# Whole float32 weights for the first expert, and a skipped branch behind its down product

## The chip, the core and the metric

The kernel runs on one core of a Trainium2 chip. A core has a matmul engine (PE, with a weight-load side PEld), a vector engine (DVE), an activation engine (ScalarE, ACT), a general engine (GpSimd, POOL), a sequencer that mostly issues transfers (SyncE, SP) and 16 DMA engines. Each engine works through its own list of instructions in order and waits on semaphores for the others. The metric is the time of one execution on the device in microseconds (us), the median of several runs.

## What is computed

Two encoder layers over 512 tokens of width 1024. Each has a norm, an input projection, four attention mixers, an output projection with a residual, and then a mixture of 16 experts, which is where the change is made. Cut to that part:

```
for layer in range(2):
    ...                                     # norm, projection, four mixers, residual
    t = rms_norm(x, norm2_g)                # 512 x 1024
    g_prob = softmax(t @ wg + bg)           # 4 groups, the best one is taken
    e_logits = (t @ we + be) of that group  # 4 experts, the best two are taken
    gate = weight of each of the 16 experts for each token
    for e in range(16):
        hid = silu(t @ w_gate[e]) * (t @ w_up[e])     # 1024 -> 512
        y = y + gate[:, e:e+1] * (hid @ w_down[e])    # 512 -> 1024
    x = x + y
```

Everything is float32.

## The kernel before, in words

**Tokens.** The routed tokens of an expert are gathered into a list of at most 96 (`CAP`). A list is made from one-hots (`oh`, DVE) and four small matmuls (`pli`), then GpSimd gathers the rows (`xg`) from a copy of `h` in memory (`h2d`), PE transposes them (`ptg`, eight of them, L1413) and they become `xh` and `xl`. Expert 0 is an exception: its input comes out of PE already transposed, from products of one-hots with `h` (`acc`, L1142). If an expert had more than 96 tokens, further rounds would follow in `overflow` (L1466): a number of rounds (`nrd`) is read by every engine, and a branch (L1478) is entered if it is over 1. With these inputs it is never entered.

**Weights.** An expert has 12 units of 512 KB (128 x 1024 float32): four of gate (`g`), four of up (`u`), four of down (`d`). `Weights.load` puts them in order on SP's queue into raw buffers (26 of them, and rows of `x_sb` when these are free). `Weights.split` makes two operands of a unit in the one-pass matmul format float32r: `hi` is a rounded copy (ACT, L144), `lo` what is left (`raw - hi`, DVE or GpSimd, L145); the raw buffer is free after `lo`. Six split units can stand at a time (`HL`): a unit's slot comes free when PE has used it (`free`). `mm3` (L268) multiplies in three one-pass matmuls: hi by `xh`, lo by `xh`, hi by `xl`, so a unit takes 6 matmuls of 512 columns.

**Order.** The units follow the list `MOE_ORDER`: 0g 0u 1g 0d 1u 2g 1d 2u 3g 2d and so on: gate of the next expert before down of this one. In the loop (L1536 to L1585) a unit is split if that has not been done, used, freed, and then further units are split up to six ahead. `silu` (ACT, L1427) follows the gate units, `hidden` (DVE, L1439, the product `sg` of silu and up) the first gate unit of the next expert, `turn_hidden` (L1448) its third; `turn` of the next expert stands inside up, and so do the list (`listed`, `start`) of the expert three ahead. `store` (ACT, L1462) scales the down product into `ye`, which GpSimd adds to the output.

**The opening.** What stands between the router and the first expert is written out by hand in `TAIL`, a table of words for each stage. The letters that matter here: `s` splits the next unit (`sV` with DVE, `sG` with GpSimd for `lo`), `T` makes expert 0's input from `acc`, `K` computes the routing weights (`weights`) and their parts, `m` clears a gather buffer, `S` starts the gather of expert 1, `O` is the overflow branch, `B` and `q` are a store and a small copy. The last stage, 69, is `T K m sG B O q sG S`. So the branch is passed before any expert, and expert 1's gather comes last.

Of the kernel before, what the change touches and what calls it, by code (L numbers as in the profile page):

```python
# [11 lines left out]
FT = mybir.dt.float32  # L12
# [7 lines left out]
S = 512  # L20
# [31 lines left out]
HOLD = 2  # L52
MIX = "gg" + "dg" * 8 + "gggggg"
# [9 lines left out]
def hybrid_encoder(ctx: ExitStack, tc: tile.TileContext, I: dict, out: bass.AP, depth=2, dbg=None):  # L63
# [83 lines left out]
    class Weights:  # L147
# [4 lines left out]
        def __init__(self):  # L152
            self.spec, self.raw, self.hl, self.where = [], {}, {}, {}
            self.loaded = self.done = self.used = 0
            self.moe_pools = []
            self.held, self.paused = 0, False
            self.spare, self.spare_upto = [], 0

# [30 lines left out]

        def split(self, upto, E=V):  # L190

            while self.done < min(upto, self.loaded) and self.done < self.used + self.HL - self.held:
# [5 lines left out]
                r = self.where.pop(u)  # L198
                if isinstance(r, bass.AP):
                    self.spare.append(r)  # L200
# [13 lines left out]
        def free(self, upto):  # L214
            for u in range(self.used, upto):
                del self.hl[u]
            self.used = upto
# [105 lines left out]
    for layer in range(depth):  # L323
# [32 lines left out]
        with ExitStack() as c2:  # L356
# [431 lines left out]
            with ExitStack() as c3:  # L788
# [356 lines left out]
                def list_rows():  # L1145

                    pl = ps.tile([128, 512], FT, name="pli", tag="tr")
                    for t in range(NT):
# [7 lines left out]
                              p=route, x=pick, s=lambda E: W.split(W.done + 1, E), w=warm)  # L1156
# [151 lines left out]
        with ExitStack() as c2:  # L1308
# [30 lines left out]
            def weights():  # L1339
# [17 lines left out]
                W.load(len(W.spec), A)  # L1357
# [20 lines left out]
            class Expert:  # L1378
# [5 lines left out]
                def lists(self, parts, rows=True, gates=True):  # L1384

                    c0, c1 = 0 if rows else 2, 5 if gates else 2
                    pl = pq.tile([128, 8], FT, name="pli", tag="pv")
# [16 lines left out]
                def turn(self, turned=None):  # L1404
                    self.xh = sm.tile([128, 8, CAP], FR, name="xh", bufs=2)
                    self.xl = sm.tile([128, 8, CAP], FR, name="xl", bufs=2)
                    for k in range(0, 8, 4):
                        if turned:
                            pt = turned[k // 4]
                        else:  # L1410
                            pt = ps.tile([128, 4, CAP], FT, name="ptg", tag="tr")
                            for j in range(4):
                                PE.transpose(pt[:, j], self.g[:CAP, (k + j) * 128:(k + j + 1) * 128], ident[:CAP, :CAP])  # L1413
# [52 lines left out]
            def overflow():  # L1466
# [11 lines left out]
                with tc.If(rounds > 1):  # L1478
                    V.memset(off, 0.0)
                    SP.dma_start(posd[0].rearrange("(t p) e -> p t e", p=128), pos)  # L1480
                    SP.dma_start(posd[1].rearrange("(t p) e -> p t e", p=128), gate)
                    with tc.For_i(1, rounds):
                        V.tensor_scalar(off, off, float(CAP), None, op0=OP.add)
                        with tc.For_i(0, NE) as e:
                            one = bass.ds(e, 1)
                            pe_ = sm.tile([128, 2, NT], FT, name="pe")
                            for j in range(2):
                                SP.dma_start(pe_[:, j], posd[j, :, one].rearrange("(t p) o -> p (t o)", p=128))
# [6 lines left out]
                            x.lists(lambda t: co[:, t])  # L1495
# [3 lines left out]
                            x.pg = ps.tile([128, FF], FT, name="pg", tag="mm")[:CAP]  # L1499
                            x.pu = pq.tile([128, FF], FT, name="pu", tag="pv")[:CAP]  # L1500
# [9 lines left out]

                            x.pd = [pool.tile([128, 512], FT, name="pd", tag=tag)[:CAP] for pool, tag in ((ps, "mm"), (pq, "pv"))]
# [10 lines left out]
            def start(e):  # L1522
# [3 lines left out]
                else:  # L1526
# [5 lines left out]
                          m=lambda: G.memset(xg[1], 0.0), S=lambda: start(1), K=weights, O=overflow,  # L1532
                          q=lambda: G.tensor_copy(parts[..., :2], tokb[:, :, None].to_broadcast([128, NT, NE, 2])))
            tail(TAIL[len(seq) + 5])
            for e, m in MOE_ORDER:
                us = wbase[layer, e, m][0]  # L1536
                for i, u in enumerate(us):
# [24 lines left out]
                    for s, todo in ((e + 3, (('u', 0), ('u', 2))),) + (((2, (('g', 2), ('u', 0))),) if e == 0 else ()):  # L1562
                        if (m, i) in todo and s < NE:
                            (start if (m, i) == todo[1] else listed)(s)
                    if (e, m) == (0, 'u') and i in (0, 2):
                        j = i // 2
                        X[j].hots = hots(j, sm.tile([128, NT, CAP], BF, name="oh", bufs=2))
                        X[j].lists(lambda t: parts[:, t, j], rows=j == 0)
# [111 lines left out]
```

## Time and profile before

| | us |
|---|---|
| runs: median (lowest, highest) of 3 | 1391.43 (1387.01, 1392.2) |
| profiled execution, its own time | 1387.39 |
| its span, first to last instruction | 1385.6 |
| PE busy | 1293.8 (93%) |
| DVE busy | 1087.5 (78%) |
| ACT busy | 876.4 (63%) |
| GpSimd busy | 358.5 (26%) |

All times in the trace count from the start of the span. The expert phases run from about 386 to 700 us and from 1062 to the end. A row of the timeline has a start, a duration, the engine, the line of the kernel, the operation, what it writes and reads, and a count; in brackets stands how long the engine had been idle and who released it. Consecutive instructions of one kind are put together, and their durations overlap, so that the distance between two is the difference of two starts. A row of stretches has the busy time of PE, PEld, DVE, ACT and GpSimd with instruction counts, then the granted clock of PE as a share of full speed, the share of the DMA engines' time and the GB/s. A row of the chain has a start, a duration and the work on which the end depended. A busy engine may be one whose instruction waits inside.

### The profile page before, as it was taken

The page shows a single profiled execution, that of the slowest core. Times are in us where ns is not written, and L with a number is a line of the kernel's source. Part 1 is how long each engine was busy: PE and PEld are TensorE (multiplying, and loading weights), DVE is VectorE, ACT ScalarE, POOL GpSimd, SP SyncE. Part 2 cuts the span into 40 slices and gives each one's busy share as a digit, 9 for nine tenths or more (in the row PEclk, how much of TensorE's full clock was granted, in tenths as well). Part 3 has the DMA queues.
Part 4 walks back from the last instruction along what each step waited for, and adds up shares of the span by engine and source line. Part 5 has one row for each costly group of instructions (what it writes and reads, how often), then busy time and mean ns, then how long its engine had stood idle before and what let it go on. Part 6 is the DMA issues. An engine that isn't in the chain of part 4 may idle for free.

```text
span 1385.6 us, 21247 instructions
## 1 busy us (share of the span) xinstructions
PE 1293.8 (93%) x7222; PEld 1013.9 (73%) x7222; DVE 1087.5 (78%) x2108; ACT 876.4 (63%) x1439; POOL 358.5 (26%) x582
## 2 busy tenths in 40 slices
PE   8998899999969999999989998999998899999996
PEld 6776688888836666766777886888886566667674
DVE  4636776878688999999876488687876799999994
ACT  3443357766357888888744454676644588888884
POOL 4204324323422111111041152431345021111120
PEclk8999999999979999999999999999997899999999
DMA  7332251012699999999454223200176899999960
GB/s 198 116 97 62 83 177 51 18 60 108 257 334 292 370 363 373 359 361 332 124 136 123 91 77 79 69 28 28 62 296 222 292 351 368 370 363 366 367 206 13
DMA packets 100575, 278.46 MB, mean 201 GB/s; under 512 B 19465, under 2 KB 30521, under 8 KB 100456
## 3 DMA queue, kind: packets, MB, share of 16 engines
q1 hardware_dynamic: 89528, 247.95, 50.4%
q0 software_dynamic: 10352, 27.41, 7.9%
q10 hardware_dynamic: 576, 1.64, 0.4%
q8 instruction: 59, 0.97, 0.3%
q14 instruction: 60, 0.49, 0.1%
HBM read 264.34 MB, written 24.81 MB: 209 GB/s over the span
## 4 chain that ended last, share of the span: by engine, by line
PE 25%; DVE 17%; DMA 12%; issue 11%; ACT 4%; POOL 1%; POOLq 0%; DVEq 0%; ACTq 0%; SPq 0%
PE pm L268 9%; DVE lo L145 7%; PE pd L268 5%; DMA raw<-in_expert_w_down_dram 4%; DMA raw<-in_expert_w_gate_dram 3%; PE ptr L276 2%; DMA raw<-in_expert_w_up_dram 2%; PE pv L911 2%; PE pu L268 2%; ACT hi L144 2%; PE pg L268 2%; DMA out_dram<-ye,ix 1%; DVE oh L341 1%; ACT ye L1462 1%; DVE xl L145 1%
## 5 line engine op out<-in xcount | busy, mean ns | idle before, releaser
L145 DVE TENSOR_TENSOR lo<-raw,hi 128x1024 fp32r<-128x1024 f32 (+2 forms) x400 | 483.6, 1230 | 68.1 <-ACT hi L144 58.3
L144 ACT ACTIVATE hi<-raw 128x1024 fp32r<-128x1024 f32 (+1 forms) x410 | 422.7, 1050 | 92.6 <-PE pu L268 20.2
L268 PE MATMUL pm<-lo,hTh 128*128 128x512 f32 (+2 forms) x384 | 137.3, 358 | 6.8 <-DVE lo L145 5.1
L268 PE MATMUL pm<-hi,hTh 128*128 128x512 f32 (+2 forms) x384 | 139.3, 363 | 3.0 <-ACT hi L144 1.5
L268 PE MATMUL pm<-hi,hTl 128*128 128x512 f32 (+2 forms) x384 | 136.9, 356 | 0.4
L268 PE MATMUL pg<-lo,xh 128*96 128x512 f32 x256 | 104.0, 406 | 5.5 <-POOL lo L145 4.0
L268 PE MATMUL pu<-hi,xh 128*96 128x512 f32 (+1 forms) x272 | 109.0, 401 | 0.0
L268 PE MATMUL pg<-hi,xh 128*96 128x512 f32 x256 | 106.2, 415 | 2.4 <-ACTq L1478 1.4
L268 PE MATMUL pd<-hi,hl 128*96 128x512 f32 x256 | 102.1, 399 | 4.5 <-DVE hl L145 4.5
L268 PE MATMUL pu<-lo,xh 128*96 128x512 f32 (+1 forms) x272 | 105.7, 388 | 0.0
L268 PE MATMUL pu<-hi,xl 128*96 128x512 f32 (+1 forms) x272 | 104.8, 385 | 0.0
L911 PE MATMUL pv<-v,pT 128*128 128x64 f32 x768 | 98.3, 271 | 6.5 <-DVE pT L899 2.7
L268 PE MATMUL pg<-hi,xl 128*96 128x512 f32 x256 | 102.9, 402 | 0.6 <-DVE E L1349 0.6
L268 PE MATMUL pd<-lo,hh 128*96 128x512 f32 x256 | 101.2, 395 | 1.6 <-DVE lo L145 1.6
L882 ACT ACTIVATE p<-p,m 128x512 f32<-128x512 f32 x96 | 68.7, 716 | 52.2 <-DVE m L864 51.9
L911 PEld LDWEIGHTS pv<-v,pT 128*128 128x128 f32 x768 | 93.5, 192 | 10.8 <-DVE pT L899 4.8
L268 PE MATMUL pd<-hi,hh 128*96 128x512 f32 x256 | 100.7, 394 | 0.0
L268 PEld LDWEIGHTS pm<-lo,hTh 128*128 128x128 f32 x384 | 73.5, 191 | 18.2 <-DVE lo L145 9.8
L268 PEld LDWEIGHTS pm<-hi,hTh 128*128 128x128 f32 x384 | 73.8, 192 | 15.4 <-ACT hTh L144 2.4
L268 PEld LDWEIGHTS pm<-hi,hTl 128*128 128x128 f32 x384 | 73.5, 192 | 11.2 <-DVE hTl L145 2.1
L276 PE MATMUL ptr<-ident,p 128*128 128x128 f32 x512 | 76.9, 272 | 0.3
L276 PEld LDWEIGHTS ptr<-ident,p 128*128 128x128 f32 x512 | 63.3, 140 | 17.8 <-DVE pT L899 1.2
(371 smaller groups left out, 2746.6 us busy)
## 6 DMA issues: line engine op xcount, KB each, us to landing
raw<-in_expert_w_down_dram SPq DMA_DIRECT2D x116, 512.0 KB
raw<-in_expert_w_gate_dram SPq DMA_DIRECT2D x114, 512.0 KB
raw<-in_expert_w_up_dram SPq DMA_DIRECT2D x112, 512.0 KB
raw<-in_w_in_dram SPq DMA_DIRECT2D x32, 512.0 KB
raw<-in_w_out_dram SPq DMA_DIRECT2D x16, 512.0 KB
toep<-brep SPq DMA_DIRECT2D x16, 448.0 KB
x_sb<-in_expert_w_gate_dram SPq DMA_DIRECT2D x14, 512.0 KB
x_sb<-in_expert_w_down_dram SPq DMA_DIRECT2D x12, 512.0 KB
```

The lines of the kernel that those rows point to most:

```text
L144: A.activation(hi, src, AF.Copy)
L145: E.tensor_tensor(lo, src, hi.bitcast(FT), op=OP.subtract)
L268: PE.matmul(pt, a, b, start=first and n == 0, stop=last and n == tot - 1)
L276: PE.transpose(pt[:c, i * 128:(i + 1) * 128], s, ident)
L341: V.tensor_scalar(oh[:, t], iota, pos[:, t, e:e + 1], None, op0=OP.is_equal)
L882: A.activation(p, p, AF.Exp, bias=m, scale=-1.0, accum_out=s)
L911: PE.matmul(st['pv'][:, t], self.pT[:, k * 128:(k + 1) * 128], self.v(k), start=k == 0, stop=k == NT - 1)
L1462: A.activation(ye[:CAP, n * 512:(n + 1) * 512], self.pd[n], AF.Copy, scale=self.w)
```

## The change

Three things are done.

1. The eight units of expert 0's gate and up are kept whole (`W.whole`): they are not split, PE multiplies the raw float32 buffer with a float32 `xh`, one matmul where there were three. `xl` of expert 0 is gone; its `xh` is two plain copies, one by ACT and one by DVE. A raw buffer of such a unit is free when PE has used it.
2. The branch is taken out of `TAIL` and stands behind expert 0's down product, `store` included; expert 1's silu comes behind it. Its inner loads are issued by ACT and not SP, and its PSUM tags change.
3. The order of the opening is changed: in stage 69 the gather of expert 1 comes first, then expert 0's input, six splits on DVE (1g and the first two of 0d) and then the routing weights; the single splits of stages 64 and 66, and all GpSimd splits of stage 69, are gone. The first lists are spread by a table `FIRST`, and the gate weights of experts 0 and 1 are listed within their own down units.

```diff
-        64: "sV d0",
+        64: "d0",
-        66: "e1 sG c2",
+        66: "e1 c2",
-        69: "T K m sG B O q sG S"}
+        69: "m S T B sV sV sV sV sV sV K q"}
+FIRST = ((2, ((0, 'u', 1), (0, 'u', 3))), (3, ((1, 'g', 1), (1, 'g', 3))), (4, ((1, 'u', 0), (1, 'u', 2))))
...
+        def next(self):
+            while self.done in self.whole and self.done < self.loaded:
+                src, k, n, moe = self.spec[self.done]
+                self.hl[self.done] = self.raw.pop(self.done).rearrange("p (k n) -> p k n", k=k)
+                self.done += 1
+            return self.done
...
         def free(self, upto):
             for u in range(self.used, upto):
                 del self.hl[u]
+                if u in self.whole:
+                    self.leave(u)
+                    self.load(len(self.spec))
...
+                if e == 0:
+                    W.whole.update(wbase[l, e, m][0])
...
+                    if turned:
+                        self.xh = self.xh.bitcast(FT)
+                        A.activation(self.xh[:, :4], turned[0], AF.Copy)
+                        V.tensor_copy(self.xh[:, 4:], turned[1])
+                        return
...
+                    if self is X[0]:
+                        for j in range(2):
+                            k = 2 * i + j
+                            PE.matmul(getattr(self, 'p' + m), self.xh[:, k], w[:, j], start=k == 0, stop=k == 7)
+                        return
...
-                    SP.dma_start(r, w)
+                    A.dma_start(r, w)
...
-                    for s, todo in ((e + 3, (('u', 0), ('u', 2))),) + (((2, (('g', 2), ('u', 0))),) if e == 0 else ()):
+                    for s, todo in FIRST if e < 2 else ((e + 3, (('u', 0), ('u', 2))),):
...
-                    if (e, m) == (0, 'u') and i in (0, 2):
+                    if m == 'd' and e < 2:
...
-                if m == 'g':
+                if m == 'g' and e != 1:
                     X[e].silu()
...
+                if (e, m) == (0, 'd'):
+                    overflow()
+                    X[1].silu()
```

The order of instructions on PE where the expert phase of a layer opens, before. `nrd` is the number of rounds, and between the two branch rows lies the body that is not entered; `pg` is the gate product, `raw` a whole unit, `hi` and `lo` its two parts.

```order
L1142 MATMUL acc<-scr,h_4155 128x96 x8
L1469 TENSOR_LOAD nrd
L1478 COMPARE_AND_BRANCH
...
L1478 UNCONDITIONAL_BRANCH
L268 MATMUL pg<-hi,xh 96x512
L268 MATMUL pg<-lo,xh 96x512
L268 MATMUL pg<-hi,xl 96x512
```

The same place of PE now; `ptg` are the transposes of expert 1's gathered rows, `pli` the list of expert 2.

```order
L1163 MATMUL acc<-scr,h_4149 128x96 x8
L1450 MATMUL pg<-raw,xh 96x512 x8
L1450 MATMUL pu<-raw,xh 96x512 x4
L1438 MATMUL ptg<-ident,xg 128x96 x8
L1450 MATMUL pu<-raw,xh 96x512 x4
L1411 LDWEIGHTS oh
L1411 MATMUL pli<-parts,oh 96x5
```

The branch is gone from between `acc` and the first gate product, and 16 matmuls with whole weights stand for 48 with halves.

ACT at its branch, before: the last rows ahead of it, and the first behind it. `DMAHW` names are the eight lanes on which loads report.

```order
L1356 ACTIVATE e_4320<-e_4320 128x4 [waits DVE_49]
L186 DMA x_sb<-in_expert_w_up_dram 128x1024 [waits DMAHW7_49,DMASW3_49]
L144 ACTIVATE hi<-raw 128x1024 [waits DMAHW6_49]
L1469 TENSOR_LOAD nrd [waits DVE_49]
L1478 COMPARE_AND_BRANCH
...
L1478 UNCONDITIONAL_BRANCH [waits Activation_49]
L144 ACT_TABLE_LOAD
L144 ACTIVATE hi<-raw 128x1024
```

ACT at its branch now, behind the down product of expert 0; `ye` is that product scaled, `sg<-pg` the silu of expert 1, `xh<-ptg` the input of expert 2.

```order
L145 ACTIVATE hi<-x_sb 128x1024 [waits DMAHW1_49,DVE_49,PE_49]
L1492 ACTIVATE ye<-pd,w 96x512 [waits DMASW1_49,DMASW0_49,DMASW2_49,DVE_49,PE_49]
L1492 ACTIVATE ye<-pd,w 96x512 [waits PE_49]
L1499 TENSOR_LOAD nrd [waits DVE_49]
L1508 COMPARE_AND_BRANCH
...
L1508 UNCONDITIONAL_BRANCH [waits Activation_49]
L1457 ACTIVATE sg<-pg 96x512 [waits DMAHW3_49,DMAHW2_49,DMAHW4_49,DMAHW1_49,DMAHW5_49,DMAHW0_49,DMAHW6_49,DVE_49,DMAHW7_49,PE_49,Activation_49]
L145 ACTIVATE hi<-x_sb 128x1024
L145 ACTIVATE hi<-raw 128x1024 [waits PE_49]
L145 ACTIVATE xh<-ptg 128x384 [waits PE_49] x2
```

Behind the branch there were splits of expert 0's units; now there is a silu that has all eight lanes in its wait.

SP at its branch now (before it had the same rows with the branch at L1478, behind the loads of two up units).

```order
L185 DMA raw<-in_expert_w_down_dram 128x1024 [waits DMAHW5_49,DVE_49]
L185 DMA x_sb<-in_expert_w_down_dram 128x1024 [waits DMAHW6_49,DVE_49]
L1499 TENSOR_LOAD nrd [waits DVE_49]
L1499 ISA x2
L1508 COMPARE_AND_BRANCH
...
L1508 UNCONDITIONAL_BRANCH [waits DMAHW0_49,DMAHW1_49,DMAHW2_49,DMAHW3_49,DMAHW4_49,DMAHW5_49,DMAHW6_49,DMAHW7_49]
L185 DMA x_sb<-in_expert_w_down_dram 128x1024 [waits DMAHW7_49,DVE_49]
L185 DMA raw<-in_expert_w_down_dram 128x1024 [waits DMAHW0_49,DVE_49]
```

The wait for the eight lanes came with the branch; the loads ahead of it are now ones that wait for DVE.

## Rows read from the trace of the kernel before

**Rows 1.** The page: busy time of engines, and two groups of instructions.

```profile
PE 1293.8 (93%) x7222; PEld 1013.9 (73%) x7222; DVE 1087.5 (78%) x2108; ACT 876.4 (63%) x1439; POOL 358.5 (26%) x582
...
L145 DVE TENSOR_TENSOR lo<-raw,hi 128x1024 fp32r<-128x1024 f32 (+2 forms) x400 | 483.6, 1230 | 68.1 <-ACT hi L144 58.3
L144 ACT ACTIVATE hi<-raw 128x1024 fp32r<-128x1024 f32 (+1 forms) x410 | 422.7, 1050 | 92.6 <-PE pu L268 20.2
```

**Rows 2.** Stretches, from layer 0's first expert to its last ones.

```profile
386.00:396.00 10.00, 6.46 (x13) 3.24 (x13) 9.19 (x24) 7.36 (x10) 5.44 (x4) 0.51 1.01 375
...
462.34:480.62 18.28, 18.09 (x89) 12.68 (x89) 16.98 (x24) 15.13 (x19) 2.75 (x2) 1.00 1.01 367
663.42:681.70 18.28, 18.28 (x89) 13.02 (x88) 16.50 (x17) 15.66 (x20) 1.44 (x1) 1.00 0.40 111
```

**Rows 3.** The chain of waits, two experts' down products near layer 0's end.

```profile
662.51 5.53 PE pd L268 x24
...
680.14 5.53 PE pd L268 x24
```

**Rows 4.** The timeline of PE, opening of the experts in both layers.

```profile
383.85 2.10 PE L1142 MATMUL acc<-scr,h 128*128 128x96 f32 x16
...
392.96 0.74 PE L268 MATMUL pg<-lo,xh 128*96 128x512 f32 x1 [1.70 <-POOL lo L145]
...
407.98 0.78 PE L1389 MATMUL pli<-parts,oh 128*96 128x5 bf16 x4 [3.28 <-DVE oh L341]
...
419.34 0.59 PE L268 MATMUL pg<-hi,xh 128*96 128x512 f32 x1
...
430.95 0.40 PE L268 MATMUL pu<-hi,xh 128*96 128x512 f32 x1
...
1058.76 3.71 PE L1142 MATMUL acc<-scr,h 128*128 128x96 f32 x16
...
1069.32 0.74 PE L268 MATMUL pg<-lo,xh 128*96 128x512 f32 x1 [1.73 <-POOL lo L145]
...
1074.73 0.57 PE L268 MATMUL pg<-hi,xh 128*96 128x512 f32 x1
...
1094.13 0.63 PE L268 MATMUL pg<-hi,xh 128*96 128x512 f32 x1
```

**Rows 5.** PE's timeline, the same transposes in windows ending at 374.6 and 374.9.

```profile
374.44 0.41 PE L276 MATMUL ptr<-ident,x_sb 128*128 128x128 f32 x2
...
374.44 0.63 PE L276 MATMUL ptr<-ident,x_sb 128*128 128x128 f32 x4
```

**Rows 6.** SP's waits at the branch: 384 to 404 and 1062 to 1080.

```profile
SPq L1478 <- SPq L1478: 5.9, 4, 2.4
...
SPq L1478 <- SPq L1478: 6.8, 1, 6.8
```

**Rows 7.** The timeline of ACT, silu of expert 0 in layer 0.

```profile
400.57 1.28 ACT L1427 ACT_TABLE_LOAD   x1 [1.88 <-SPq L1478]
401.86 0.59 ACT L1427 ACTIVATE sg<-pg 96x512 f32<-96x512 f32 x1
```

**Rows 8.** The chain of waits, three loads: start, us to landing.

```profile
586.40 3.28 DMA raw<-in_expert_w_up_dram
...
1066.52 6.41 DMA raw<-in_expert_w_up_dram
...
1219.52 13.89 DMA raw<-in_expert_w_down_dram
```

**Rows 9.** The timeline of DVE: routing weights' end, expert 1's sequence, both anchors.

```profile
390.33 0.26 DVE L1334 CAST parts<-gate 128x64 bf16<-128x64 f32 x1
...
432.94 1.23 DVE L145 TENSOR_TENSOR lo<-x_sb,hi 128x1024 fp32r<-128x1024 f32 x1 [0.86 <-ACT hi L144]
...
439.46 0.68 DVE L1439 TENSOR_TENSOR sg<-sg,pu 96x512 f32<-96x512 f32 x1
...
1114.73 0.68 DVE L1439 TENSOR_TENSOR sg<-sg,pu 96x512 f32<-96x512 f32 x1
```

More of the change, by code (lines that the diff above doesn't have):

```diff
@@ L157, in __init__ @@
             self.spare, self.spare_upto = [], 0
+            self.whole = set()
         def add(self, src, k, n, moe=False):
@@ L188, in load, with room_for, leave @@
                 self.loaded += 1
+        def room_for(self):
+            return sum(u not in self.whole for u in range(self.used, self.done)) < self.HL - self.held
+        def next(self):
[4 more added lines that the diff above has]
+            return self.done
+        def leave(self, u):
+            r = self.where.pop(u)
+            if isinstance(r, bass.AP):
+                self.spare.append(r)
         def split(self, upto, E=V):
-            while self.done < min(upto, self.loaded) and self.done < self.used + self.HL - self.held:
+            while self.next() < min(upto, self.loaded) and self.room_for():
                 u = self.done
@@ L1155, in hybrid_encoder @@
                 STAGES = dict(l=list_rows, b=norm_pair, c=turn_pair, o=open_out, d=close_out, e=turn_x, r=norm_x, f=logits, h=normed,
-                              p=route, x=pick, s=lambda E: W.split(W.done + 1, E), w=warm)
+                              p=route, x=pick, s=lambda E: W.split(W.next() + 1, E), w=warm)
                 def tail(words):
@@ L1356, in weights @@
                 A.activation(e2, e2, AF.Exp)
-                W.load(len(W.spec), A)
+                W.load(len(W.spec))
                 gw = sm.tile([128, NT], FT, name="gw")
@@ L1382, in __init__, with lists @@
                     self.g, self.hots = g, hots
-                def lists(self, parts, rows=True, gates=True):
+                def lists(self, parts, rows=True, gates=True, room=None):
                     c0, c1 = 0 if rows else 2, 5 if gates else 2
-                    pl = pq.tile([128, 8], FT, name="pli", tag="pv")
+                    pool, tag = room or (pq, "pv")
+                    pl = pool.tile([128, 8], FT, name="pli", tag=tag)
                     for t in range(NT):
@@ L1405, in turn @@
                     self.xh = sm.tile([128, 8, CAP], FR, name="xh", bufs=2)
+                    if turned:
[3 more added lines that the diff above has]
+                        return
                     self.xl = sm.tile([128, 8, CAP], FR, name="xl", bufs=2)
                     for k in range(0, 8, 4):
[L1408 to L1413, printed above, removed]
+                        pt = ps.tile([128, 4, CAP], FT, name="ptg", tag="tr")
+                        for j in range(4):
+                            PE.transpose(pt[:, j], self.g[:CAP, (k + j) * 128:(k + j + 1) * 128], ident[:CAP, :CAP])
                         split(self.xh[:, k:k + 4], self.xl[:, k:k + 4], pt)
@@ L1479, in overflow @@
                     V.memset(off, 0.0)
-                    SP.dma_start(posd[0].rearrange("(t p) e -> p t e", p=128), pos)
-                    SP.dma_start(posd[1].rearrange("(t p) e -> p t e", p=128), gate)
+                    A.dma_start(posd[0].rearrange("(t p) e -> p t e", p=128), pos)
+                    A.dma_start(posd[1].rearrange("(t p) e -> p t e", p=128), gate)
                     with tc.For_i(1, rounds):
@@ L1494, in overflow @@
                                        [one_hot(pe_[:, 0, t:t + 1]) for t in range(NT)])
-                            x.lists(lambda t: co[:, t])
+                            x.lists(lambda t: co[:, t], room=(ps, "tr"))
                             V.memset(x.g, 0.0)
@@ L1509, in overflow @@
                             x.turn_hidden()
-                            x.pd = [pool.tile([128, 512], FT, name="pd", tag=tag)[:CAP] for pool, tag in ((ps, "mm"), (pq, "pv"))]
+                            x.pd = [pq.tile([128, 512], FT, name="pd", tag="sc")[:CAP] for _ in range(2)]
                             for n in range(2):
@@ L1531, in hybrid_encoder @@
             STAGES.update(T=lambda: X[0].turn(late['acc']), B=lambda: G.dma_start(stream[:, NT - 1], x_sb[:, NT - 1]),
-                          m=lambda: G.memset(xg[1], 0.0), S=lambda: start(1), K=weights, O=overflow,
+                          m=lambda: G.memset(xg[1], 0.0), S=lambda: start(1), K=weights,
                           q=lambda: G.tensor_copy(parts[..., :2], tokb[:, :, None].to_broadcast([128, NT, NE, 2])))
@@ L1561, in hybrid_encoder @@
                         X[e + 1].turn()
-                    for s, todo in ((e + 3, (('u', 0), ('u', 2))),) + (((2, (('g', 2), ('u', 0))),) if e == 0 else ()):
-                        if (m, i) in todo and s < NE:
-                            (start if (m, i) == todo[1] else listed)(s)
-                    if (e, m) == (0, 'u') and i in (0, 2):
-                        j = i // 2
-                        X[j].hots = hots(j, sm.tile([128, NT, CAP], BF, name="oh", bufs=2))
-                        X[j].lists(lambda t: parts[:, t, j], rows=j == 0)
+                    for s, todo in FIRST if e < 2 else ((e + 3, (('u', 0), ('u', 2))),):
+                        if e > 1:
+                            todo = [(e,) + w for w in todo]
+                        if (e, m, i) in todo and s < NE:
+                            (start if (e, m, i) == todo[1] else listed)(s)
+                    if m == 'd' and e < 2:
+                        if i == 0:
+                            X[e].hots = hots(e, sm.tile([128, NT, CAP], BF, name="oh", bufs=2))
+                        elif i == 2:
+                            X[e].lists(lambda t: parts[:, t, e], rows=e == 0)
                     if m == 'g' and i == 0 and e == NE - 1 and not last:
```

9 lines of the change are left out of this document (3 added, 6 removed).

## Prediction

> **What bounds the kernel now.** I read the page's busy shares first: the matmul engine PE is busy 93% of the span [rows 1], which says little about where an edit would pay. So I cut the first expert phase into stretches [rows 2]. From 386 to 396 us PE is busy only 6.46 of 10 us, at a granted clock of 0.51, the lower of its two levels (1.2 GHz of 2.4), while VectorE (DVE) is busy 9.19. In the steady part each expert takes 18.28 us. PE looks full there (18.09), but the page warns that a busy PE may be one that waits, so I set its work against the end of the layer, where the chain of waits holds PE alone: from one expert's 24 down matmuls at 662.51 to the next one's at 680.14 it takes 17.63 us [rows 3]. The steady period, 0.65 us longer, is thus set by DVE's chain of `lo` subtractions and the gate product `sg`; time that the start of the phase saves is kept only if it brings DVE's sequence forward. My anchor is DVE's `sg` of expert 1 (silu times up): 439.46 us in layer 0, 1114.73 in layer 1 [rows 9]. From there on both kernels run the same program, so the shifts of the anchors are what the change is worth.
>
> Before the anchor PE waits for the operands of expert 0: for GpSimd's `lo` 1.70 us at 392.96, for one-hots 3.28 us at 407.98. Expert 1's first gate matmul comes at 419.34 (layer 1: 1094.13), its up at 430.95 [rows 4]. The phase opens at 386.0, where the 16 `acc` pieces (383.85 + 2.10) end.
>
> **The change, part by part.** *Expert 0 whole.* It removes 48 one-pass matmuls and 8 splits (8 `hi` of ScalarE, ACT; 8 `lo`, two of them on GpSimd), and puts 16 ordinary float32 matmuls of 512 columns in their place. No such matmul is in the trace. `acc` is one with 96 columns; its 8 matmuls per half stand as 16 pieces, so I take two passes. Two more 128-column float32 transposes cost 0.63 - 0.41 = 0.22 us [rows 5], 0.11 each; four times that is 0.44 for 512 columns, 0.88 a matmul in two passes, 14.1 us for 16. The bounds: one pass would cost 7.0; `acc`'s 2.10 / 16 = 0.131 per 96 columns, scaled by columns, gives 0.70 a pass and 22.4 us. I take 14.1, because in `acc` weight loads of 128 columns stand beside short passes, and a pass of 512 columns covers them.
>
> The Trainium skill weighs against this: "TensorE: Matmul & The Clock Gate", the table of terms, calls the transpose mode four times faster for FP32. If plain passes took four times what the transposes of the trace take, the 16 would cost an estimated 56 us; `acc` with 0.131 us for 96 columns [rows 4], hardly more than a transpose, speaks against it, so I give that no chance.
>
> The clock: `acc` takes 3.71 us in layer 1, where the clock is low, against 2.10 [rows 4]; matmuls of 512 columns I take at double, 1.76. In layer 1 the matmuls came back to full at 1074.73, 5.4 us after the last wait of over a microsecond, which ended at 1069.32 [rows 4]. After the change PE has no operand to wait for: the raw units have long landed, and `xh` needs two plain copies. I take 6 us at the low level: 6 / 1.76 = 3.4 matmuls, then 12.6 x 0.88 = 11.1, together 17.1. With eight transposes of xg (0.9 by the same 0.11) and four list matmuls (0.2) expert 1's gate starts 18.2 after the opening, at 404.2 instead of 419.34. Gate 1 and down 0 took 430.95 - 419.34 = 11.6; with two more list groups (0.3) they end at 416.1. The six splits ahead (6 x 1.23 on DVE [rows 1]) and the routing weights behind them (they ran from 387 to past 390.33 [rows 9], some 5 us with their parts) end near 399 and hide behind the float32 matmuls; the first to need them is the list of expert 2 near 404, so their cover is 5 us.
>
> *The branch moved.* It is never entered, yet each engine loads a number and jumps. SP, which issues the weight loads, must also see its outstanding loads land before it may pass: 5.9 us of waits in layer 0, 6.8 in layer 1 [rows 6], and ACT's silu waited for it, 1.88 us [rows 7]. The change puts the inner loads on ACT's queue, but in the new order SP's row behind the branch still waits for all eight load lanes, and so does ACT's silu of expert 1. Queued behind that silu on ACT are the next `hi` and the transposed input; behind those DVE's `lo`, one-hots, `xl` and the anchor, and PE's list matmuls within up 1. How late is the silu? DVE's last `lo` before the branch is that of 2g0: its slot comes free with the third unit of down 0, near 414.6, and `hi` 1.05 and `lo` 1.23 [rows 1] end it near 417.2. It frees the buffer of the last load, issued near 417.5. At the branch of layer 1 a load took 6.41 us to land; in the steady parts one took 3.28 and one 13.89 [rows 8]. I take 4.8, the middle of 6.41 and 3.28, since SP's queue is thin while it waits for buffers. So SP and ACT go on near 422.6, with a guess of 0.3 for the jump. ACT's own road, two `ye` and the branch behind 416.1, ends near 419.6: the drain comes last.
>
> For the same time the Trainium skill has a sum: "DMA: Bandwidth & Descriptors", on the two cost components, 2.0 us plus bytes over 436 GB/s, an estimate of 3.2 us for 512 KB. By that the silu comes 1.6 us earlier in each layer and the total 3 us lower; the 6.41 us [rows 8] speaks against it.
>
> From silu to anchor: silu 0.59, one `hi` 1.05, then DVE's sequence that the trace has in the same order, 439.46 - 432.94 = 6.5 [rows 1, 7, 9]; 8.2 in all. Anchor 0 comes at 430.8 instead of 439.46: 8.7 gained. Layer 1 opens at 1058.76 + 3.71 = 1062.5; the same steps give gate 1 at 1080.7 (against 1094.13), down 0's end at 1092.6, the silu at 1099.1, the anchor at 1107.3 against 1114.73: 7.4 gained. PE idles some 4 us at the list matmuls while ACT waits and may lose its clock by that; I charge 0.5 us a layer, as DVE and not PE sets the pace.
>
> *The rest.* Loads that PE now releases come no later than DVE released them. PE's own jump I charge at nothing, since PE waits behind it anyway; without that cover it is a fraction of a microsecond. The spread lists and the lost GpSimd splits take work off DVE's crowded start and cost nothing.
>
> **Sum:** 8.7 + 7.4 - 1.0 = 15.1 us, 1.1%. On the profiled execution of 1387.39 (span 1385.6) that is 1372; on the median of the runs, 1391.43, 4 us above it, which I forecast for, 1376.
>
> **The rivals.** (a) *The drain costs little.* If the last load lands in 3.28 us or goes out before `lo` of 2g0, the silu comes at ACT's own 419.6, 3 us earlier a layer; with a clock that rises 2 us sooner (1 us a layer) it is 8 in all: gain 23, 1368. For it: the 3.28. Against: the 6.41, measured at the branch.
> (b) *The drain is as long as the longest landings.* Ten us instead of 4.8 takes 5.2 a layer; gain 5, 1386. For it: 13.89. Against: the 6.41, again.
> (c) *The gain is not kept.* SP, held at the branch, issues late, and splits wait for loads later: 1391. Against: by 663 to 682 us the DMA share has fallen to 0.40 [rows 2], so loads run well ahead.
> (d) *The other side: the clock stays low through the whole float32 stretch.* PE is fed without a gap, but float32 passes may not raise its clock: in layer 1 `acc` ran 3.71 us without a gap and did not. Then 16 x 1.76 = 28.2 us instead of 17.1, 11.1 later a layer: layer 0 loses 2.4, layer 1 3.7, and the low clock that runs on into gate 1 some 1.5 each. 9 us in all, 1400. It decides from 21 to 23 us of low clock: the stretch takes 14.1 + t/2 with t us at the low level, and the gains of 7.4 and 8.7 are gone 14.8 and 17.4 us past the 6. For it: that row. Against: `acc` at 383.85 and the transposes at full clock [rows 4, 5].
> That the change doesn't do what it says has no weight: the new order has the 16 matmuls, and the branch behind down 0.
>
> **How the numbers follow.** Forecast 0.54, (a) 0.20, (b) 0.11, (c) 0.06, (d) 0.09. A measurement of this kernel can tell about 0.5%, 7 us, from no change. Faster by more: the forecast and (a), 0.74; within: (b) and (c), 0.17; slower: (d), 0.09. The range goes from (a) taken from the profiled execution and one us more, 1363, to (b), 1387; above it lie (c) and (d), 0.15, below it 0.05. The 22.4 us bound of the float32 price would cost 8 us a layer and land at (c).
>
> **What would show it.** Right: `pg` and `pu` pieces 0.44 us apart after some 6 us at twice that; gate 1 near 404 and 1081; SP waiting about 5 us at the branch and ACT's silu 6 us behind down 0; anchors near 431 and 1107; the period still 18.28. Wrong: all pieces at 0.88 (d), no wait of ACT at the branch (a), one of 10 us (b), `hi` waiting for loads or a longer period (c).

## The result and the profile after

The changed kernel takes 1396.88 us (median of 12 runs) against 1390.01 for the kernel before (12 runs): a ratio of 1.0061, 95% interval 1.0050 to 1.0071. It is slower by 0.6%. The forecast was 1376, with a range of 1363 to 1387: wrong in sign and outside the range. The profiled execution has a span of 1393.8 us, 8.2 more than before.

The first step held to within 1.5 us. PE's timeline of the changed kernel (start, duration, engine, line, operation, count; in brackets idle time and who ended it), layer 0 and then layer 1:

```profile
385.39 2.00 PE L1163 MATMUL acc<-scr,h 128*128 128x96 f32 x16
387.23 7.03 PE L1450 MATMUL pg<-raw,xh 128*96 128x512 f32 x16
394.10 3.60 PE L1450 MATMUL pu<-raw,xh 128*96 128x512 f32 x8
401.28 1.51 PE L1438 MATMUL ptg<-ident,xg 96*128 96x96 f32 x8 [3.59 <-DMA xg<-h2d,nrd]
402.58 4.62 PE L1450 MATMUL pu<-raw,xh 128*96 128x512 f32 x8
...
407.21 0.45 PE L289 MATMUL pg<-hi,xh 128*96 128x512 f32 x1
...
419.71 0.44 PE L289 MATMUL pu<-hi,xh 128*96 128x512 f32 x1 [0.36 <-PEq L1508]
...
438.25 0.78 PE L1411 MATMUL pli<-parts,oh 128*96 128x5 bf16 x4 [13.49 <-DVE oh L362]
...
1063.78 3.71 PE L1163 MATMUL acc<-scr,h 128*128 128x96 f32 x16
1067.29 8.50 PE L1450 MATMUL pg<-raw,xh 128*96 128x512 f32 x16
...
1084.35 0.46 PE L289 MATMUL pg<-hi,xh 128*96 128x512 f32 x1
...
1116.27 0.78 PE L1411 MATMUL pli<-parts,oh 128*96 128x5 bf16 x4 [14.43 <-DVE oh L362]
```

The 16 pieces of `pg` take 7.03 us, from 387.23 to the first of `pu` at 394.10 (0.43 each, 0.86 a matmul), at the full clock. Expert 1's first gate matmul stands at 407.21 (419.34 before, [rows 4]) and its up at 419.71 (430.95). Counted from the end of `acc`, the gate comes 13.6 us earlier in layer 0 and 14.8 in layer 1. Then the line of `pli` in up 1 says where all of it went: PE sits idle 13.49 us, and 14.43 in layer 1, waiting for DVE's one-hots. DVE in turn waits for ACT, and then come the anchors, the `sg` of expert 1 (DVE's timeline):

```profile
436.79 1.23 DVE L146 TENSOR_TENSOR lo<-x_sb,hi 128x1024 fp32r<-128x1024 f32 x1 [16.22 <-ACT hi L145]
...
443.31 0.68 DVE L1469 TENSOR_TENSOR sg<-sg,pu 96x512 f32<-96x512 f32 x1
...
1121.32 0.68 DVE L1469 TENSOR_TENSOR sg<-sg,pu 96x512 f32<-96x512 f32 x1
```

The anchors are at 443.31 and 1121.32, where the forecast had 430.8 and 1107.3 and the kernel before 439.46 and 1114.73 [rows 9]. ACT, in the same two places:

```profile
419.52 1.26 ACT L1492 ACTIVATE ye<-pd,w 96x512 f32<-96x512 f32 x2 [0.71 <-PEq L1508]
435.22 0.59 ACT L1457 ACTIVATE sg<-pg 96x512 f32<-96x512 f32 x1 [14.44 <-SPq L1508]
...
1113.24 0.59 ACT L1457 ACTIVATE sg<-pg 96x512 f32<-96x512 f32 x1 [15.31 <-SPq L1508]
```

Behind the two `ye` ACT is idle 14.44 us and 15.31 us ahead of the silu of expert 1, released by SP at the branch (L1508). Before, the silu at the branch waited 1.88 us [rows 7]. SP's own timeline shows why it takes so long:

```profile
395.16 3.39 SPq L188 DMA_DIRECT2D raw<-in_expert_w_gate_dram  x4
400.04 5.61 SPq L185 DMA_DIRECT2D raw<-in_expert_w_down_dram  x4
407.51 4.18 SPq L188 DMA_DIRECT2D raw<-in_expert_w_up_dram  x4
413.11 5.23 SPq L188 DMA_DIRECT2D raw<-in_expert_w_gate_dram  x4
419.15 0.33 SPq L185 DMA_DIRECT2D raw<-in_expert_w_down_dram  x1
420.60 17.79 SPq L185 DMA_DIRECT2D x_sb<-in_expert_w_down_dram  x2
```

SP issues its last load ahead of the branch at 420.60; ACT's silu starts at 435.22. So that load, and those still under way in front of it, took 14.6 us to land, where the forecast took 4.8. How much was under way stands in the DMA view of a stretch (packets, MB and share of the 16 engines' time of `q1`, the queue of SP's loads). The first row is the changed kernel from that load to the silu; the other two are the kernel before, from the last load ahead of its branch to the end of SP's waits there (392.94 to 400.4 us in layer 0, 1069.29 to 1077.6 in layer 1):

```profile
q1 hardware_dynamic: 957, 3.46, 63.4%
...
q1 hardware_dynamic: 427, 1.55, 59.9%
...
q1 hardware_dynamic: 369, 1.32, 48.6%
```

With 0.52 MB to a unit, 6.6 units still had to move in the changed kernel, and 3.0 and 2.5 in the kernel before. The stretches of the changed kernel (busy time of PE, PEld, DVE, ACT, GpSimd; then the granted clock, the DMA share and the GB/s):

```profile
386.00:396.00 10.00, 10.00 (x34) 4.66 (x33) 8.62 (x18) 6.38 (x8) 2.98 (x3) 1.00 0.99 381
396.00:406.00 10.00, 6.41 (x18) 3.00 (x17) 5.11 (x23) 3.06 (x5) 0.00 (x0) 0.83 1.02 376
406.00:420.00 14.00, 13.64 (x69) 9.03 (x68) 10.89 (x26) 8.29 (x9) 2.27 (x2) 1.00 1.03 382
420.00:438.00 18.00, 4.76 (x26) 3.22 (x24) 1.78 (x3) 3.56 (x7) 1.52 (x1) 0.74 0.69 238
```

From 386 to 420 us the DMA engines are at 0.99 to 1.03 of their time and move some 380 GB/s; at that rate a unit of 512 KB takes an estimated 1.4 us. Before, the shares in 396:406 and 406:420 were 0.78 and 0.88. Then SP is held, the queue runs dry, and the share falls to 0.69. The steady period is unchanged: PE's small wait within the down product recurs after 18.27 us (467.22 to 485.49), against 18.28 [rows 2].

By these marks the 8.2 us of the span are: 1.4 ahead of the opening of layer 0 (a stretch whose length differs between kernels here by more than that, without a cause in the change), 2.4 from the opening to the anchor in layer 0, 1.2 from there to the opening of layer 1, 1.6 to its anchor, 1.6 to the end. PE's idle wait also cost it its clock: the up matmuls behind it stand 0.43 us apart (438.89 to 441.55), and the next anchor comes 19.30 us later, where before it came after 18.28.

### The profile page after: what moved, and what is told of

It reads as the page before. It is cut to its first block, busy times and chain, and to the rows that moved or that the text cites. A ratio compares the mean times of both kernels' runs of the same rounds, so it can differ in the third digit from the quotient of the medians.

```text
span 1393.8 us, 21114 instructions
## 1 busy us (share of the span) xinstructions
PE 1289.0 (92%) x7190; PEld 1004.6 (72%) x7190; DVE 1061.2 (76%) x2094; ACT 857.4 (62%) x1419; POOL 364.6 (26%) x578
## 5 line engine op out<-in xcount | busy, mean ns | idle before, releaser
L146 DVE TENSOR_TENSOR lo<-raw,hi 128x1024 fp32r<-128x1024 f32 (+1 forms) x388 | 468.7, 1231 | 63.0 <-ACT hi L145 55.8
L145 ACT ACTIVATE hi<-raw 128x1024 fp32r<-128x1024 f32 (+1 forms) x394 | 406.3, 1050 | 97.1 <-PE pg L289 18.8
L289 PE MATMUL pu<-hi,xh 128*96 128x512 f32 (+1 forms) x256 | 101.2, 395 | 0.7 <-PEq L1508 0.7
L289 PE MATMUL pu<-lo,xh 128*96 128x512 f32 (+1 forms) x256 | 98.0, 383 | 0.0
L289 PE MATMUL pu<-hi,xl 128*96 128x512 f32 (+1 forms) x256 | 98.0, 383 | 0.0
L289 PE MATMUL pg<-hi,xh 128*96 128x512 f32 x240 | 96.9, 404 | 0.0
L289 PE MATMUL pg<-lo,xh 128*96 128x512 f32 x240 | 95.0, 396 | 0.0
L289 PE MATMUL pg<-hi,xl 128*96 128x512 f32 x240 | 94.6, 394 | 0.0
```

The lines of the kernel that those rows point to most:

```text
L145: A.activation(hi, src, AF.Copy)
L146: E.tensor_tensor(lo, src, hi.bitcast(FT), op=OP.subtract)
L289: PE.matmul(pt, a, b, start=first and n == 0, stop=last and n == tot - 1)
```

## The experiments

Theory D: the whole gain, and more, went into the wait for SP's loads under way at the branch, at a place where the queue is full. Rivals: a branch costs the same wherever it stands (F); the float32 matmuls or the lists cost it (P); loads come late (L). All ratios are to the kernel before, in the same chip session; its median was 1388.07, 1387.77 and 1387.85 us in the three sessions.

| run | edit to the changed kernel | median us | ratio (95%) |
|---|---|---|---|
| e1 | no branch | 1363.53 | 0.9836 (0.9817 to 0.9856) |
| e2 | the kernel before, no branch | 1387.67 | 1.0010 (0.9993 to 1.0027) |
| e3 | loads held from 1g | 1373.56 | 0.9897 (0.9881 to 0.9914) |
| e5 | branch behind expert 13 | 1373.63 | 0.9906 (0.9889 to 0.9922) |
| e4 | expert 0 split again | 1399.39 | 1.0093 (1.0070 to 1.0117) |
| e6 | inner loads on GpSimd | 1389.19 | 1.0004 (0.9993 to 1.0015) |
| e8 | loads held from 0u2 | 1369.12 | 0.9863 (0.9829 to 0.9896) |
| e9 | branch ahead of all experts | 1373.02 | 0.9905 (0.9883 to 0.9927) |
| e7 | inner loads on SP | 1397.16 | 1.0069 (1.0052 to 1.0085) |
| e10 | expert 0 split again, no branch | 1373.75 | 0.9898 (0.9882 to 0.9915) |
| e11 | e9 with inner loads on SP | 1360.26 | 0.9798 (0.9776 to 0.9819) |
| e12 | e8 with inner loads on SP | 1367.18 | 0.9867 (0.9841 to 0.9893) |

### Without the branch: e1 and e2

```diff
                 if (e, m) == (0, 'd'):
-                    overflow()
                     X[1].silu()
```

> The changed kernel without the overflow branch (never entered with these inputs); that part is left out. Theory D (drain): the time went into the wait for SP's eight outstanding loads at the branch, 14.4 us in layer 0 and 15.3 in layer 1 in front of ACT's silu of expert 1. Without it the silu comes some 15 us earlier in each layer and the gate product sg of expert 1 near 428 and 1092 (443.31 and 1121.32 in the changed kernel); total 1365 to 1370. Rival P (the float32 matmuls, the spread lists or a longer period cost the time): still 1385 or more.

In e2 the letter `O` is taken out of the last stage of the kernel before.

> The kernel before without the overflow branch, which is left out. Theory D: the branch cost the kernel before something too, but little, as fewer loads are under way at its place: 1.9 us of ACT and the waits for GpSimd's lo behind its own jump, 2 to 4 us a layer; 1382 to 1386. Rival F (a branch costs a fixed amount wherever it stands, some 15 us a layer): 1360. The difference between this and the changed kernel without a branch is what whole float32 weights and the new order are worth: 14 to 18 us by D.

In e1 ACT's silu of expert 1 starts without a wait, and the anchors (DVE) follow, 4 and 6 us earlier than expected:

```profile
416.20 0.59 ACT L1457 ACTIVATE sg<-pg 96x512 f32<-96x512 f32 x1
```

```profile
424.28 0.67 DVE L1469 TENSOR_TENSOR sg<-sg,pu 96x512 f32<-96x512 f32 x1
...
1086.39 0.67 DVE L1469 TENSOR_TENSOR sg<-sg,pu 96x512 f32<-96x512 f32 x1
```

From the end of `acc` to the anchor it is 38.7 us in layer 0 and 38.9 in layer 1, where the kernel before has 53.5 and 52.3: 14.8 and 13.4 us gained; the total gains 24.5 us (the profiled run, 1358.62, was the fastest of four), a little more than expected. This is the change without its drain, and it is faster by 1.6%. In the kernel before, the branch costs nothing that can be measured (0.9993 to 1.0027; less than the 2 to 4 us a layer expected). So F and P fall: the same branch (but for the queue of its inner loads, on which see e7) costs 0 at the old place and some 31 to 33 us at the new one (0.9836 to 1.0061, or 1363.5 to 1396.9).

### Loads held back ahead of the branch: e3 and e8

In e8 the unit is (0, 'u', 2).

```diff
+HOLDAT = (1, 'g', 0)
...
                 for i, u in enumerate(us):
+                    if (e, m, i) == HOLDAT:
+                        W.paused = True
...
                     overflow()
                     X[1].silu()
+                    W.paused = False
+                    W.load(len(W.spec))
```

> The changed kernel, but SP issues no load from the first gate unit of expert 1 (near 407) until behind the branch. Theory D: the queue of eight loads, 12 to 15 us from issue to landing, runs empty by 419 to 421, so SP's wait and the wait of ACT's silu fall to 1 to 3 us and the total to 1368 to 1373; the 10 loads held back are caught up, since loads run 40 us ahead. Rival F: the wait stays at 14 us, 1397. Rival L (loads become late): no wait at the branch, but splits wait for loads later, 1380 to 1397.

> As e3, but loads are held from the third up unit of expert 0 (near 401) instead of the first gate unit of expert 1: the last load ahead of the branch lands near 413, before SP gets there. Theory D: SP's wait under 1 us and ACT's silu 1 us behind ye instead of 5.6 (layer 0) and 4.6 (layer 1); 1364 to 1370. Rival L (held loads come late for their splits): no wait at the branch, but 1373 or more.

e3, SP and then ACT: the last load ahead of the branch goes out at 407.94, and the silu of expert 1 starts at 423.69, with a wait of 5.58 us (4.56 in layer 1).

```profile
407.94 0.33 SPq L189 DMA_DIRECT2D raw<-in_expert_w_up_dram  x1
```

```profile
423.69 0.59 ACT L1458 ACTIVATE sg<-pg 96x512 f32<-96x512 f32 x1 [5.58 <-SPq L1509]
...
1092.54 0.59 ACT L1458 ACTIVATE sg<-pg 96x512 f32<-96x512 f32 x1 [4.56 <-SPq L1509]
```

From that load to the silu it is again 15.7 us, so the queue is no shorter; but the drain starts earlier, and 10 us of it now lie beside the matmuls of gate 1 and down 0. The wait is longer than the 1 to 3 us expected: the last loads ahead of the hold went out only by 407.94, and took longer than the 12 to 15 us reckoned. In e8 two loads fewer go out, the last at 406.62, and SP is no longer what ACT waits for in layer 0:

```profile
418.77 1.26 ACT L1493 ACTIVATE ye<-pd,w 96x512 f32<-96x512 f32 x2 [0.71 <-DMA xg<-h2d,ix]
422.83 0.59 ACT L1458 ACTIVATE sg<-pg 96x512 f32<-96x512 f32 x1 [2.80 <-PE ptg L1439]
...
1089.30 0.59 ACT L1458 ACTIVATE sg<-pg 96x512 f32<-96x512 f32 x1 [0.70 <-SPq L1509]
```

2.80 us remain there (named after PE, which had long been done; see J below) and 0.70 in layer 1. The total is 14.5 us under the kernel before in e3 and 18.7 in e8. Seven loads in e3 and nine in e8 are held back until behind the branch; L had 1373 or more for e8, and it falls as the main cause. That the held loads cost nothing at all is not shown, since e8 is 5.6 us above e1.

### The branch late in the phase: e5

```diff
+OVAT = 13
...
-                if m == 'g' and e != 1:
+                if m == 'g' and e != OVAT + 1:
...
-                if (e, m) == (0, 'd'):
+                if (e, m) == (OVAT, 'd'):
                     overflow()
-                    X[1].silu()
+                    X[OVAT + 1].silu()
```

> The changed kernel with the branch behind expert 13's down product instead of expert 0's, silu of expert 14 behind it. There the DMA engines are at 0.4 of their time in layer 0 and at 0.09 in layer 1. Theory D: no wait of over 3 us in layer 1, up to 8 in layer 0 if loads of the next layer are on their way; 1367 to 1378. Rival F: the wait is as long there, 14 us a layer, 1397.

```profile
1328.93 0.59 ACT L1458 ACTIVATE sg<-pg 96x512 f32<-96x512 f32 x1 [3.79 <-SPq L1509]
```

In layer 1 ACT's silu of expert 14 still waits 3.79 us for SP, more than the 3 expected, and there PE is the bound, so it counts: what the kernel had gained on the kernel before shrinks there by 5 us in layer 0 and 4 in layer 1. The total, 1373.6, is within what was expected, no better than e3. The queue was not thin at this place: the DMA engines were busy 0.91 of their time from 1300 to 1320 us, and SP's waits lasted from its compare at 1320.6 to 1328.8. The share of 0.09 in the expectation belongs to a later stretch, behind the last loads, so e5 shows a shorter drain in a late place and not an empty queue.

### Expert 0 split again: e4 and e10

```diff
                 if e == 0:
-                    W.whole.update(wbase[l, e, m][0])
```

with `turn` and `gu` as before; e10 has no branch besides.

> The changed kernel with expert 0's gate and up split again (48 one-pass matmuls, 8 more splits on ACT and DVE); branch, lists and queues as changed. Theory D: expert 1's gate comes back to 415 or later, so the same loads have some 10 us more to land before the branch; the queue at the branch is thinner and ACT's silu waits 4 to 8 us there instead of 14.4. What the whole weights gain is thus mostly what the drain takes: total 1386 to 1398, near the changed kernel. Rival F (the wait is 14 us whatever runs ahead of it): over 1405. Rival P (float32 matmuls are what costs): under 1380.

> The kernel e4 (expert 0 split again, everything else as changed) without the overflow branch, which is left out. It splits the 24 us between the kernel before and the changed kernel, both without a branch, into the new order and the whole weights. In e4 expert 1's gate came 11.6 us earlier than before, in the changed kernel 13.7, both by their own opening; so D expects that the order (six splits ahead, no GpSimd splits, spread lists) carries most of it: 1367 to 1374, and whole weights the other 4 to 8 us. Rival W (the whole weights carry it): 1380 or more.

e4, ACT's silu of expert 1 in both layers, and two stretches:

```profile
434.48 0.59 ACT L1447 ACTIVATE sg<-pg 96x512 f32<-96x512 f32 x1 [10.49 <-SPq L1498]
...
1114.34 0.59 ACT L1447 ACTIVATE sg<-pg 96x512 f32<-96x512 f32 x1 [11.24 <-SPq L1498]
```

```profile
396.00:406.00 10.00, 7.35 (x36) 4.76 (x34) 9.52 (x28) 8.81 (x13) 0.00 (x0) 1.00 1.01 394
406.00:424.00 18.00, 16.58 (x69) 11.42 (x70) 16.74 (x35) 10.82 (x12) 4.29 (x2) 0.81 1.01 362
```

The wait is 10.49 and 11.24 us, longer than the 4 to 8 expected and just past the range of the total: the new order alone already keeps the DMA engines at 1.01, though the last load ahead of the branch takes 10.7 us there (423.80 to 434.48) and not 14.6. With the branch there, whole weights gain 2 to 4 us, hardly clear of the noise (1399.39 to 1396.88; 1.0093 to 1.0061); without it they gain 9 to 10 (1373.75 to 1363.53; 0.9898 to 0.9836), more than the 4 to 8 expected, and the order 14 to 16 (1387.67 to 1373.75; 1.0010 to 0.9898). So most of what whole weights save at the opening goes into a longer drain.

### Whose lanes: e6 and e7

All inner loads of the branch are issued by GpSimd in e6 (the diff shows one of them), by SP in e7.

```diff
-                    A.dma_start(r, w)
+                    G.dma_start(r, w)
```

> The changed kernel with the branch's inner loads issued by GpSimd instead of ACT. In its order SP has no wait behind the branch any more, and silu of expert 1 waits for GpSimd's lanes. Theory D, finer: the wait comes from the queue whose lanes the unentered body uses. SP's wait is 0; ACT's silu now waits for GpSimd's last transfer, the store of expert 0's rows, 9.4 us from issue to landing in the changed kernel: some 8 to 10 us instead of 14.4, total 1383 to 1390. Rival F: the wait stays 14 us, 1397.

> The changed kernel with the branch's inner loads back on SP's queue, as before the change. Theory D with J: two costs stand at the branch; the drain of SP's loads (14.4 and 15.3 us in front of ACT's silu) and, hidden under it, ACT's own jump, 6.0 us in layer 0 of the changed kernel (420.1 to 426.1) where it was 0.5 before and 0.7 with the loads on GpSimd, since ACT's unentered body is twice as long with loads in it. With the loads on SP the jump falls under 1 us but the drain stays: total as the changed kernel, 1394 to 1399. Rival Q (the ACT queue is what costs): under 1390.

In e6 SP has no wait behind the branch, and ACT's silu waits for GpSimd's transfers in its place:

```profile
433.82 0.59 ACT L1457 ACTIVATE sg<-pg 96x512 f32<-96x512 f32 x1 [10.05 <-DMA x_sb<-h2d,ix]
...
1110.65 0.59 ACT L1457 ACTIVATE sg<-pg 96x512 f32<-96x512 f32 x1 [11.33 <-DMA out_dram<-x_sb]
```

10.05 and 11.33 us, for a gather and a store: with SP not held at the branch, these share DMA engines that are busy 0.94 of their time from 420 to 434 us. The total is that of the kernel before (1.0004). In e7, with the loads on SP's queue as they were before, the wait is as in the changed kernel:

```profile
435.93 0.59 ACT L1457 ACTIVATE sg<-pg 96x512 f32<-96x512 f32 x1 [16.03 <-SPq L1508]
...
1115.88 0.59 ACT L1457 ACTIVATE sg<-pg 96x512 f32<-96x512 f32 x1 [12.85 <-SPq L1508]
```

16.03 and 12.85 us, and the total 1.0069 against 1.0061. So ACT's queue is not the cause; which engine issues the inner loads only sets which transfers must have landed.

### The branch ahead of all experts: e9, e11, e12

```diff
-        69: "m S T B sV sV sV sV sV sV K q"}
+        69: "m T O S B sV sV sV sV sV sV K q"}
...
-                if (e, m) == (0, 'd'):
-                    overflow()
-                    X[1].silu()
```

> The changed kernel with the branch back ahead of all experts (between expert 0's input and the six splits), inner loads on ACT. Theory D: SP drains some 8 loads there too, but what waits for it is ACT's silu of expert 0, which has about 10 us of float32 matmuls in front of it; the cost is a jump on PE (up to 1 us) and a table load on ACT. Sum: the kernel without a branch, 1363.5, plus 1 to 2 us a layer, 1364 to 1369. Rival F: 14 us a layer wherever it stands, 1390 or more.

e9 missed: 1373, not 1364 to 1369. PE's first float32 matmul waits for ACT, and the rows of the branch's line (duration min, median, max in ns, then first and last start in us) say for what:

```profile
393.10 9.24 PE L1450 MATMUL pg<-raw,xh 128*96 128x512 f32 x16 [5.06 <-ACTq L1508]
```

```profile
L1508 ACTq COMPARE_BRANCH  x2: 45/48/50, 387.7 to 1053.4; - x2
...
L1508 ACTq EVENT_SEMAPHORE  x2: 17/17/17, 393.0 to 1058.7; - x2
```

ACT compares at 387.7 and is behind the branch at 393.0: its jump took 5.3 us in each layer. In the changed kernel it is there too, under the drain:

```profile
L1508 ACTq COMPARE_BRANCH  x2: 45/48/50, 420.1 to 1097.1; - x2
...
L1508 SPq COMPARE_BRANCH  x2: 50/52/53, 421.8 to 1099.9; - x2
L1508 ACTq EVENT_SEMAPHORE  x2: 17/17/17, 426.1 to 1098.8; - x2
```

420.1 to 426.1 in layer 0, 1097.1 to 1098.8 in layer 1. In layer 0 of the kernel before it was 0.5, and in e6 and e7, with the loads elsewhere, 0.7. With the loads in it, ACT's unentered body is about twice as long. The jump also explains the 2.80 us left in layer 0 of e8 (419.4 to 422.4, while the last of SP's waits ended at 419.7). In e3 it runs beside the drain (417.4 to 422.4, SP's last wait ended at 423.6) and adds nothing. This became theory J, the jump, and e11 and e12 put the inner loads of e9 and e8 on SP's queue.

> As e9 (branch ahead of all experts), inner loads on SP instead of ACT. In e9 PE waited 5.06 and 4.78 us for ACT, whose jump took from 387.7 to 393.0. Theory J: with the shorter body ACT's jump takes under 1 us, PE starts some 4 us earlier in each layer: 1362 to 1368, and SP's drain is hidden behind the float32 matmuls. Rival: the jump is as long, 1373.

> As e8 (loads held from the third up unit of expert 0), inner loads on SP instead of ACT. In e8 ACT's jump took 3.0 us in layer 0 and 0.8 in layer 1. Theory J: under 1 us in both, total 2 to 3 us below e8, 1364 to 1368. Rival: as e8, 1369.

```profile
L1508 ACTq COMPARE_BRANCH  x2: 45/45/45, 388.3 to 1049.6; - x2
...
L1508 ACTq EVENT_SEMAPHORE  x2: 17/17/17, 388.7 to 1050.0; - x2
...
  PE pg L1450: 0.6, 2
```

```profile
427.18 0.68 DVE L1469 TENSOR_TENSOR sg<-sg,pu 96x512 f32<-96x512 f32 x1
...
1087.30 0.68 DVE L1469 TENSOR_TENSOR sg<-sg,pu 96x512 f32<-96x512 f32 x1
```

In e11 the jump takes 0.4 us, and PE waits 0.6 us in all for the branch. SP still waits there (from 393.3 to 399.8 us in layer 0), but what stands behind its drain is the silu of expert 0, with the float32 matmuls ahead of it; and the queue is short at this place, with 1.29 MB moved on `q1` from 392 to 399.8. The anchors are 38.5 and 37.1 us behind `acc`, no later than without a branch. The median of 1360.26 us, 2.0% under the kernel before and below the 1362 to 1368 expected, is the lowest of all kernels here. In e12 the jump fell to 0.7 and 0.9 us, but in layer 0 ACT then waited 1.49 us for SP. Its median is 2 us below that of e8, as expected; the ratios, 0.9867 and 0.9863, show no gain, so in the total J is shown by e9 and e11 alone.

## Why the prediction was wrong, point by point

**What bounds the kernel.** Right. The period stayed (18.27 against 18.28), and the shifts of the anchors are the result up to 2.8 us in the two rests behind them and the 1.4 ahead of the opening.

**Expert 0 whole.** Right in the main. 0.43 us a piece, where 0.44 was taken from the transposes; the rule of the Trainium skill that was weighed there ("TensorE: Matmul & The Clock Gate", the table of terms, four times for FP32) does not describe plain float32 matmuls here: 7.03 us for 8 of them, not 28. The 6 us at the low clock were too many: none in the first 24 pieces of layer 0 (16 in 7.03, 8 in 3.60), some 3 in layer 1 (8.50, 1.5 more than at full speed). "After the change PE has no operand to wait for" was wrong, and gave that back: PE waited 3.59 us for the gather of expert 1 ahead of 401.28, which no step had, and its last 8 pieces then took 4.62 us instead of 3.60, with the granted clock at 0.83 from 396 to 406 us. In sum, gate 1 came 13.6 and 14.8 us earlier, where the forecast had 15.1 and 13.4.

**The branch moved.** This is the step that failed. Its mechanism was right to the engine: SP's eight lanes, ACT's silu behind them, PE's list matmuls behind that, and the 8.2 us from silu to anchor (435.22 to 443.31, 8.1). The term was mis-sized by a factor of three: 4.8 us from the last load's issue to the silu, 14.6 and 14.3 in the trace. The sentence at fault is "since SP's queue is thin while it waits for buffers". It held for the kernel before (3.0 and 2.5 units to move), and even there the landing was misread: the 6.41 us belong to the last load but one, while from the last one to the end of SP's waits it was 7.5 us in layer 0 and 8.3 in layer 1. In the changed kernel the queue had 6.6 units to move. For the same change frees buffers faster (eight whole units, released by PE at 1.7 us each, and six splits early; e4 shows that the order alone fills the engines), so loads go out faster: the DMA share behind 396 us rose from 0.78 and 0.88 to 1.02 and 1.03. A load issued behind others lands when all of them have. Rival (b) named this end with the row of 13.89 us [rows 8] and took 10; it got 0.11 since the 6.41 was held against it. The DMA share of 1.01 in 386 to 396 [rows 2] was there to be read.

The other rule weighed there, "DMA: Bandwidth & Descriptors" of the Trainium skill, on the two cost components, gives an estimate of 3.2 us for one load of 512 KB; the last load ahead of the branch took over four times that. No run here shows a load alone, so the rule itself is not tried; as a price for this wait it is no use.

**The sum and the rivals.** 8.7 + 7.4 gained became 2.4 + 1.6 lost: 11.1 and 9.0 us apart, of which the drain (9.8 and 9.5 longer than forecast) is nearly all. (a) was what e1 and e11 reached by other means. (c) did not happen, with the period as before. Nor did (d), the rival on the slower side: in layer 0 the clock was full until PE had to wait for the gather, and in layer 1 it rose within the float32 stretch. The kernel became slower by the mechanism of (b), priced too low to cross zero.

**ACT's jump** was charged with 0.3 us; it took 6.0 and 1.7, hidden behind the drain, and showed only where the drain ended first (layer 0 of e8, e9).

## What to carry to other kernels

A branch that is never entered can still wait, as here, for the transfers under way on the lanes that its body uses; price it by the depth of the queue in the kernel as it will be, not as it was, and put it where its waiter has work in front of it. An edit that speeds up the consumer of a stream also fills the stream's queue: whatever drains that queue gets dearer by the same edit. Before paying for a long body on an engine that others wait for, look at that engine's own jump.

## What the runs showed of the hardware that was not expected

A jump over a body that is not entered is not always short. On ACT it took 0.4 to 0.9 us in both layers without the inner loads in its body (before, e6, e7, e11, e12). With them, in a body about twice as long, it took 3.0 to 6.5 us in layer 0 and 0.5 to 1.7 in layer 1 (changed, e3, e4, e5, e8), and 5.3 in both in e9. The Trainium skill ("Runtime: NRT & Kernel Launch", instruction fetch mechanics) says that a taken branch to a target outside the current window of pages has to fetch its page first. A long body that sometimes costs and a short one that never does agree with that, but do not show it. The DMA view has four packets of instructions within e9's jump (387.7 to 393.0); it has four in e11 as well, from 388.3 to 393.3, when ACT's jump had ended, so whose they are is not known. Length was not tried apart from the loads themselves, nor why the same body costs more in layer 0; it stays open whether its place in the pages or the load on the DMA engines decides.

Whole float32 matmuls of 512 columns with 96 output rows stand in the trace as two pieces of 0.43 us at the full clock, 0.86 in all, beside 0.69 for the three one-pass matmuls (3 x 0.23 [rows 3]) that they replace: 1.25 times the PE time, and no splits. The clock also rose while PE ran only these: in layer 1 `acc` still ran at the low level (3.71 us), and the granted clock was 0.86 from 1068 to 1076 us and 1.00 from 1076 to 1084. Where PE waits for splits, as at this opening, that is worth 9 to 10 us in two layers (e10 to e1).
